# First 16 scores of each token found in the score stage, and 54 instead of 60 expert blocks ahead

## The chip, the cores and the metric

One core of one Trainium2 chip runs the whole program in one launch. The metric is device time in microseconds (us): 3645.66 us is the median of three runs before the change (3639.0 to 3648.67).

The engines are PE (TensorE matmul; PEld its weight loads), DVE (VectorE), ACT (ScalarE), POOL (GpSimd) and SP (SyncE, which only issues DMAs here). Each has its own instruction stream, runs it in order, and waits on semaphores for the others.

## The reference, cut to what matters

Two transformer blocks on 512 tokens of width 1024. All of the change lies in the last part, the PEER layer (a product-key mixture of 16384 experts):

```
def one(xb):                                   # 128 tokens
    q = (xb @ w_pq).reshape(128, 8, 2, 128)
    s = einsum('thpd,hpkd->thpk', q, sub_keys)             # 16 score rows of 128 keys per token
    sv, si = top_k(s, 16)                                  # "the first 16 scores"
    cand = sv[:, :, 0, :, None] + sv[:, :, 1, None, :]
    cidx = si[:, :, 0, :, None] * 128 + si[:, :, 1, None, :]
    best, pos = top_k(cand, 16)
    eidx = take_along_axis(cidx, pos);  g = softmax(best)
    act = gelu(einsum('thkd,td->thk', expert_u[eidx], xb))
    return einsum('thk,thkd->td', g * act, expert_v[eidx])
```

Here t is the token, h one of 8 heads, p the half of the key, k the key.

## The kernel before, in words

Matmuls are made of three: an f32 operand is split into hi and lo parts, and hi*hi, lo*hi and hi*lo are added in PSUM (lines 124 to 126). A weight tile of 128x1024 (512 KB) comes from DRAM into a ring of six `raw` buffers (`wload`, line 114), ACT casts the hi part (`whi`, line 117), and DVE or POOL subtracts it for the lo part (`wlo`, line 118). `whi` and `wlo` have three buffers each.

PEER has three stages.

- **The score stage** (`scores`). 16 blocks of `w_pq` are projected (24 matmuls of 512 columns each). `keys(m, q)` multiplies each q with its 128 sub-keys (four matmuls, one for each tile of 128 tokens), ACT copies the scores from PSUM to `psc`, and they are written to DRAM (`scd`). From the fifth block on, the residual is transposed and stored beside it.
- **The route stage** (`route`, with `up` beside it). For each of the four token tiles the 2048 scores of a token are read back (`sc`), and `top16` finds the first 16 of each of the 16 rows: MAX8, FIND_INDEX8, MATCH_REPLACE8, MAX8, FIND_INDEX8, all on DVE. Then come 50 candidate sums per head, their 16 best (`v3`), and `pick`, which turns positions into expert numbers (fi, fj) and gates. For tile 0 the expert rows themselves are gathered later. For tiles 1 to 3 the gates become dense: 32 groups a tile, each of four tokens, in which DVE writes one-hots `oj` and `oi` (for one group in four ACT scales `oi`) and PE multiplies them; ACT copies the result to `stage`. The generator yields at places where `peer` then writes an expert block ahead (`up`): projection of tiles 1 to 3 with `uT[i]` (24 matmuls of 384 columns), Gelu on ACT, result to DRAM (`actd`). NPRE = 60 blocks are done so. The 20 blocks that belong to top16's yields have their `wlo` subtraction on POOL, the other 40 on DVE.
- **The main loop**, 128 iterations. Iteration i multiplies the gated activations of block i with `v[i]` (`down`, 18 matmuls of 512 columns). An activation is either read back (`mixed`, i < NPRE; called a plain iteration below) or computed then with `up` two iterations ahead (called a mixed iteration: 42 matmuls). Beside it the 256 gathered rows of tile 0 (128 of u, 128 of v, 512 KB each for 128 tokens, in the same `raw` ring) are fetched by POOL's indirect DMAs and reduced on DVE: one an iteration up to NPRE, and the rest spread evenly over what is left (`want`).

The order of instructions on each engine is made by the framework's scheduler when the program is built; the source gives what depends on what, and the buffers. Memory pools matter too: `pe` (which holds `act` and `stage`) is opened after `pq`, the score stage's pool, is closed, and takes its place in SBUF.

Of the kernel before, what the change touches and what calls it, by code (L numbers as in the profile page):

```python
# [7 lines left out]
F32 = mybir.dt.float32  # L8
F32R = mybir.dt.float32r
I32 = mybir.dt.int32  # L10
U32 = mybir.dt.uint32
# [4 lines left out]
P = 128  # L16
# [11 lines left out]
class Kern:  # L28
# [1536 lines left out]
    def peer(self, h, first, residual, done):  # L1565

        nc, a = self.nc, self.a
        mod = self.mod2
        hhi, hlo = h
        with ExitStack() as c:  # L1570
            p0 = self.pool(c, "pe0")
            h0 = self.h0 = self.t(p0, [P, D], "h0")
            with ExitStack() as c1:
                qp = self.pool(c1, "pq")
                self.sk = self.t(qp, [P, 16, P], "sk")
                nc.sync.dma_start(self.sk, a["sk"])
                self.scores(qp, hhi, hlo, first, residual)
                done()
            pp = self.pool(c, "pe")
            self.stage = self.t(pp, [P, 2, P, 64], "stage")  # L1580
            with ExitStack() as c2:
                rp = self.pool(c2, "pr")
                self.iota16 = self.t(rp, [P, 16], "iota")
                nc.sync.dma_start(self.iota16, a["iota16"])
                self.iota = self.t(rp, [P, P], "iota128")
                nc.sync.dma_start(self.iota, a["iota128"])
                self.row0 = self.t(rp, [P, 16], "row0")
                nc.sync.dma_start(self.row0, a["row0"])
                jobs = self.route(rp, pp)
                pre = 0  # L1590
                for n, eng in jobs:
                    for _ in range(n):
                        if pre < self.NPRE:
                            self.up(pp, pre, hhi, hlo, eng)
                            pre += 1
# [27 lines left out]
            for t in range(4):  # L1623
                for i in range(2):
                    s = slice(512 * i, 512 * i + 512)
# [3 lines left out]
                    else:  # L1629
                        z = self.raw()[:, :512]  # L1630
# [3 lines left out]

    NPRE = 60
    PROD = 5
# [9 lines left out]
    def scores(self, p, hhi, hlo, first, residual):  # L1646

        nc, a = self.nc, self.a

        def keys(m, q):  # L1650
            pk = self.mm_ps()
            for t in range(4):
                nc.tensor.matmul(pk[:, t * P : t * P + P], q[:, t * P : t * P + P], self.sk[:, m], start=True, stop=True)
            s = self.t(p, [P, 4, P], "psc", bufs=2)
            nc.scalar.copy(s, pk.rearrange("p (t k) -> p t k", t=4))
            nc.sync.dma_start(a["scd"].rearrange("t p m k -> p t m k")[:, :, m], s)

        h = list(zip(hhi, hlo))
        qs = [self.t(p, [P, S], "pq", bufs=3) for _ in first]
        self.halves(first, h, lambda n, ps, cs: nc.scalar.copy(qs[n][:, cs], ps[:, cs]), lambda i: None)  # L1660
        last = list(enumerate(qs))
        norm = self.last_hi, self.last_split
        for m in range(len(first), 16):
            with self.after(*norm):
                w = self.cut(*self.wload(a["w_pq"][m]))
            ps = self.mm_ps()
            self.proj_feat(w, h, ps)
            for z in last:
                keys(*z)
            q = self.t(p, [P, S], "pq", bufs=3)  # L1670
            nc.scalar.copy(q, ps)
            last = [(m, q)]
            if 4 <= m < 12:
                with self.after(*norm):
                    residual(m - 4)
        keys(*last[0])
# [10 lines left out]
    def route(self, p, pp):  # L1687

        nc, a = self.nc, self.a
        dve, pool = nc.vector, nc.gpsimd  # L1690
        for t in range(4):
            sc = self.t(p, [P, 16, P], "sc", bufs=1)
            nc.sync.dma_start(sc, a["scd"][t])
            sv = self.t(p, [P, 16, 16], "sv", bufs=1)
            si = self.t(p, [P, 16, 16], "si", U32, bufs=1)
            for m in range(16):
                self.top16(p, sc[:, m], P, sv[:, m], si[:, m], "v2")
                if m % 4 == 3:
                    yield 1 + (t == 0), pool
            sf = self.t(p, [P, 16, 16], "sf", bufs=1)  # L1700
# [14 lines left out]
            for h in range(8):  # L1715
                self.top16(p, cand[:, h], 50, best[:, h], pos[:, h], "v3")
            yield 2, dve
            pf = self.t(p, [P, 8, 16], "pf", bufs=1)
# [19 lines left out]
            self.pick(p, pf, self.iota16, f4[:, :, 1], fj, ALU.is_equal)  # L1738
            yield 2, dve
            g = self.t(pp, [P, 8, 16], "gate0") if t == 0 else self.t(p, [P, 8, 16], "gate", bufs=1)  # L1740
            nc.vector.tensor_sub(g, best, best[:, :, 0:1].to_broadcast([P, 8, 16]))
            nc.scalar.activation(g, g, AF.Exp)
            s = self.t(p, [P, 8], "gs", bufs=1)
# [11 lines left out]
            tp = self.sc_ps()  # L1755
# [3 lines left out]
            for b in range(32):  # L1759
# [18 lines left out]
                if b % 4 == 3:  # L1778
                    yield 1, dve
                if t < 3 and b % 16 == 15:  # L1780
# [100 lines left out]
    def scratch(self):  # L1881
# [3 lines left out]
        self.a["growd"] = dp.tile([1, D], F32, tag="growd", name="growd")  # L1885
        self.a["scd"] = dp.tile([4, P, 16, P], F32, tag="scd", name="scd")
        self.a["gd"] = dp.tile([4, P, P, 64], F32, tag="gd", name="gd")
# [152 lines left out]
```

## Time and profile before

| | |
|---|---|
| median of the runs | 3645.66 us |
| profiled execution, its own time | 3644.18 us |
| its span (first to last instruction) | 3642.1 us |
| busy share of the span: PE, PEld, DVE, ACT, POOL | 96%, 83%, 72%, 44%, 21% |
| moved from and to HBM | 566.66 MB read, 41.18 MB written |

The profiled execution lies 1.5 us under the median. PE is busy nearly all the time, but a busy PE is not PE at its peak: matmuls are pipelined, so what counts is how many of them a stretch holds. The stages of PEER by the trace: the score stage ends at 2371 us, the route stage at 2759 us, the main loop at about 3634 us.

### The profile page before, as it was taken

What the parts mean: (1) busy time and instruction counts of PE and PEld (TensorE: products, weight loads), DVE (VectorE), ACT (ScalarE), POOL (GpSimd) and SP (SyncE); (2) the same over time, 40 slices, a digit from 0 to 9 for tenths busy, and PEclk for the clock granted to TensorE, in tenths of its full rate; (3) what the DMA queues carried; (4) which work ended last, traced back from release to release, by engine and by line L of the source; (5) the groups of instructions that cost most, each with busy time, mean ns of one, the idle gap of its engine ahead of it and who ended that gap; (6) DMA issues with size and microseconds to landing.
All of it is one profiled execution on the core that took longest, in us unless ns stands there. A gap on an engine that the chain in (4) does not pass through costs nothing.

```text
span 3642.1 us, 53180 instructions
## 1 busy us (share of the span) xinstructions
PE 3505.6 (96%) x19035; PEld 3036.0 (83%) x19035; DVE 2624.4 (72%) x6192; ACT 1590.9 (44%) x3137; POOL 774.2 (21%) x890
## 2 busy tenths in 40 slices
PE   6999999999999999999999999999988999999998
PEld 5899888888888987888888768889987888788787
DVE  6788677874478864488736675189998887777777
ACT  4676533413367754342334554334554333333332
POOL 4223101000232320010012212021101223333232
PEclk9999999999999999999999999999999999999999
DMA  5211266673321122446632112455556998888887
GB/s 197 70 37 56 77 202 203 219 237 103 107 70 60 53 70 70 143 147 219 204 122 65 56 39 102 140 175 165 200 180 219 336 329 290 294 308 301 294 290 267
DMA packets 228821, 611.33 MB, mean 168 GB/s; under 512 B 24070, under 2 KB 89638, under 8 KB 225868
## 3 DMA queue, kind: packets, MB, share of 16 engines
q1 hardware_dynamic: 191692, 473.69, 39.1%
q0 software_dynamic: 36864, 134.23, 11.1%
q8 instruction: 150, 2.46, 0.3%
q14 instruction: 115, 0.94, 0.1%
HBM read 566.66 MB, written 41.18 MB: 167 GB/s over the span
## 4 chain that ended last, share of the span: by engine, by line
PE 67%; DVE 13%; DMA 12%; ACT 4%; issue 3%; POOL 0%; SPq 0%; DVEq 0%; ACTq 0%; POOLq 0%
PE mm L124 16%; PE mm L125 16%; PE mm L126 16%; DMA raw<-uT 8%; DVE wlo L118 4%; DMA raw<-v 3%; ACT whi L117 3%; PE pv L552 1%; DVE oi L1773 1%; PE tr L126 1%; PE tr L124 1%; PE tr L125 1%; PE sc L496 1%; PE mm L1775 1%; DVE oj L1765 1%
## 5 line engine op out<-in xcount | busy, mean ns | idle before, releaser
L117 ACT CAST whi<-raw 128x1024 fp32r<-128x1024 f32 (+2 forms) x603 | 610.2, 1015 | 1153.5 <-PE mm L125 411.5
L118 DVE TENSOR_TENSOR wlo<-raw,whi 128x1024 fp32r<-128x1024 f32 (+2 forms) x583 | 686.8, 1180 | 445.6 <-ACT whi L117 383.6
L126 PE MATMUL tr<-hhi,wlo 128*128 128x384 f32 x1024 | 356.4, 348 | 24.1 <-DVE wlo L118 23.7
L124 PE MATMUL tr<-hhi,whi 128*128 128x384 f32 x1024 | 353.0, 345 | 18.0 <-ACT whi L117 13.6
L124 PE MATMUL mm<-hhi,whi 128*128 128x512 f32 (+1 forms) x976 | 366.6, 376 | 0.2 <-ACT mr L746 0.2
L125 PE MATMUL mm<-hlo,whi 128*128 128x512 f32 (+1 forms) x976 | 363.6, 373 | 1.8 <-DVE hlo L153 1.2
L126 PE MATMUL mm<-hhi,wlo 128*128 128x512 f32 (+1 forms) x976 | 363.2, 372 | 0.0
L125 PE MATMUL tr<-hlo,whi 128*128 128x384 f32 x1024 | 349.4, 341 | 0.0
L124 PE MATMUL mm<-whi,hhi 128*128 128x384 f32 (+2 forms) x896 | 308.6, 345 | 21.1 <-ACT hhi L152 13.7
L229 DVE CUSTOM_DVE_ANT_0 adaj<-adaw,cr 128x256 f32<-128x256 f32 x620 | 271.5, 438 | 57.4 <-DMA adaw<-ada_w 43.8
L125 PE MATMUL mm<-wlo,hhi 128*128 128x384 f32 (+2 forms) x896 | 308.4, 344 | 2.8 <-DVE wlo L118 2.8
L126 PE MATMUL mm<-whi,hlo 128*128 128x384 f32 (+2 forms) x896 | 305.9, 342 | 0.0
L282 POOL TENSOR_TENSOR nsum<-nsum,nsq 128x256 f32<-128x256 f32 x78 | 68.9, 887 | 1099.7 <-ACT nsq L280 1098.1
L1848 POOL DMA_INDIRECT raw<-u,idx x128 | 144.9, 1132 | 460.1 <-DVE act L1856 320.3
L126 PEld LDWEIGHTS tr<-hhi,wlo 128*128 128x128 f32 x1024 | 196.0, 191 | 40.9 <-DVE wlo L118 39.7
L124 PEld LDWEIGHTS tr<-hhi,whi 128*128 128x128 f32 x1024 | 196.4, 192 | 31.1 <-ACT whi L117 23.4
L125 PEld LDWEIGHTS mm<-hlo,whi 128*128 128x128 f32 x976 | 183.8, 188 | 34.0 <-DVE hlo L153 1.7
L124 PEld LDWEIGHTS mm<-hhi,whi 128*128 128x128 f32 x976 | 183.6, 188 | 33.5 <-issue 0.7
L126 PEld LDWEIGHTS mm<-hhi,wlo 128*128 128x128 f32 x976 | 183.7, 188 | 32.5 <-issue 0.3
L124 PEld LDWEIGHTS mm<-whi,hhi 128*128 128x128 f32 x896 | 171.6, 191 | 37.2 <-ACT hhi L152 13.8
L125 PE MATMUL mm<-wlo,ewh 128*128 128x512 f32 x512 | 201.4, 393 | 0.0
L126 PE MATMUL mm<-whi,ewl 128*128 128x512 f32 x512 | 199.6, 392 | 0.0
(602 smaller groups left out, 8390.1 us busy)
## 6 DMA issues: line engine op xcount, KB each, us to landing
adaw<-ada_w SPq DMA_DIRECT2D x139, 512.0 KB
raw<-uT SPq DMA_DIRECT2D x128, 512.0 KB
raw<-v SPq DMA_DIRECT2D x128, 512.0 KB
raw<-w_up SPq DMA_DIRECT2D x64, 512.0 KB
raw<-w_dn SPq DMA_DIRECT2D x64, 512.0 KB
raw<-w_b SPq DMA_DIRECT2D x48, 384.0 KB
raw<-w_aqk SPq DMA_DIRECT2D x32, 512.0 KB
raw<-w_g SPq DMA_DIRECT2D x32, 512.0 KB
```

The source lines that it names most:

```text
L117: nc.scalar.copy(hi[:, :n], raw[:, :n])
L118: self.last_lo = (eng or nc.vector).tensor_sub(lo[:, :n], raw[:, :n], hi[:, :n])
L124: mm(ps, ah, bh, start=start, stop=False)
L125: mm(ps, ah, bl, start=False, stop=False)
L126: mm(ps, al, bh, start=False, stop=stop)
L229: nc.vector.tensor_tensor_reduce(junk, wt[:, q * 256 : q * 256 + 256], cond[:, q * 256 : q * 256 + 256], op0=ALU.mult, op1=ALU.add, scale= ...
L282: add_ins = (nc.vector if k == 7 else nc.gpsimd).tensor_add(tot, tot, sq)
L496: self.nc.tensor.matmul(ps, q, hi, start=True, stop=False)
L552: nc.tensor.matmul(po[:, cols], wT[:, kt], v[:, kt, hl * P : hl * P + P], start=(kt == 0), stop=(kt == 3))
L1765: nc.vector.tensor_tensor(oj, io, cb(1), ALU.is_equal)
L1773: nc.vector.tensor_scalar(oi[:, n], self.iota, one(0), one(2), ALU.is_equal, ALU.mult)
L1848: nc.gpsimd.indirect_dma_start(z, None, src, bass.IndirectOffsetOnAxis(ap=idx[:, k % P : k % P + 1], axis=0))
```

## The change

`psc` is no longer written to DRAM and read back. `keys` calls `top16` on the four tiles of `psc` as soon as they are in SBUF, and the results of all four tiles are kept in `tops`. The sub-keys come in 16 loads of 64 KB (three buffers) in place of one of 1 MB. The `wlo` subtractions of `w_pq` (14 of the 16 blocks) go from DVE to POOL, those of all `up` blocks to DVE. NPRE is 54, the yields hand out 6, 14, 14 and 20 blocks to the four tiles, and the pool `pe` lies on the other side of SBUF.

```diff
--- before.py
+++ after.py
@@ -1570,15 +1570,16 @@
         with ExitStack() as c:
             p0 = self.pool(c, "pe0")
             h0 = self.h0 = self.t(p0, [P, D], "h0")
+            c2 = ExitStack()
+            tp = self.pool(c2, "pt")
+            self.tops = [(self.t(tp, [P, 16, 16], "sv", bufs=4), self.t(tp, [P, 16, 16], "si", U32, bufs=4)) for _ in range(4)]
             with ExitStack() as c1:
                 qp = self.pool(c1, "pq")
-                self.sk = self.t(qp, [P, 16, P], "sk")
-                nc.sync.dma_start(self.sk, a["sk"])
                 self.scores(qp, hhi, hlo, first, residual)
                 done()
-            pp = self.pool(c, "pe")
+            pp = self.pool(c, "pe", side="right")
             self.stage = self.t(pp, [P, 2, P, 64], "stage")
-            with ExitStack() as c2:
+            with c2:
                 rp = self.pool(c2, "pr")
                 self.iota16 = self.t(rp, [P, 16], "iota")
                 nc.sync.dma_start(self.iota16, a["iota16"])
@@ -1588,10 +1589,10 @@
                 nc.sync.dma_start(self.row0, a["row0"])
                 jobs = self.route(rp, pp)
                 pre = 0
-                for n, eng in jobs:
+                for n in jobs:
                     for _ in range(n):
                         if pre < self.NPRE:
-                            self.up(pp, pre, hhi, hlo, eng)
+                            self.up(pp, pre, hhi, hlo)
                             pre += 1
             while pre < self.NPRE:
                 self.up(pp, pre, hhi, hlo)
@@ -1632,7 +1633,7 @@
                         (nc.vector if 2 * t + i > 4 else nc.gpsimd).tensor_add(xt[t][:, s], xt[t][:, s], z)
                     nc.sync.dma_start(a["out"][t * P : t * P + P, s], xt[t][:, s])
 
-    NPRE = 60
+    NPRE = 54
     PROD = 5
     BOUND = (6, 14), (3, 8)
     BOUND2 = (6, 14), (8, 17)
@@ -1649,11 +1650,14 @@
 
         def keys(m, q):
             pk = self.mm_ps()
+            sk = self.t(p, [P, P], "sk", bufs=3)
+            nc.sync.dma_start(sk, a["sk"][:, m])
             for t in range(4):
-                nc.tensor.matmul(pk[:, t * P : t * P + P], q[:, t * P : t * P + P], self.sk[:, m], start=True, stop=True)
+                nc.tensor.matmul(pk[:, t * P : t * P + P], q[:, t * P : t * P + P], sk, start=True, stop=True)
             s = self.t(p, [P, 4, P], "psc", bufs=2)
             nc.scalar.copy(s, pk.rearrange("p (t k) -> p t k", t=4))
-            nc.sync.dma_start(a["scd"].rearrange("t p m k -> p t m k")[:, :, m], s)
+            for t in range(4):
+                self.top16(p, s[:, t], P, *(z[:, m] for z in self.tops[t]), "v2")
 
         h = list(zip(hhi, hlo))
         qs = [self.t(p, [P, S], "pq", bufs=3) for _ in first]
@@ -1662,7 +1666,7 @@
         norm = self.last_hi, self.last_split
         for m in range(len(first), 16):
             with self.after(*norm):
-                w = self.cut(*self.wload(a["w_pq"][m]))
+                w = self.cut(*self.wload(a["w_pq"][m], eng=nc.gpsimd))
             ps = self.mm_ps()
             self.proj_feat(w, h, ps)
             for z in last:
@@ -1687,16 +1691,8 @@
     def route(self, p, pp):
 
         nc, a = self.nc, self.a
-        dve, pool = nc.vector, nc.gpsimd
         for t in range(4):
-            sc = self.t(p, [P, 16, P], "sc", bufs=1)
-            nc.sync.dma_start(sc, a["scd"][t])
-            sv = self.t(p, [P, 16, 16], "sv", bufs=1)
-            si = self.t(p, [P, 16, 16], "si", U32, bufs=1)
-            for m in range(16):
-                self.top16(p, sc[:, m], P, sv[:, m], si[:, m], "v2")
-                if m % 4 == 3:
-                    yield 1 + (t == 0), pool
+            sv, si = self.tops[t]
             sf = self.t(p, [P, 16, 16], "sf", bufs=1)
             nc.vector.tensor_copy(sf, si)
 
@@ -1714,7 +1710,7 @@
             pos = self.t(p, [P, 8, 16], "pos", U32, bufs=1)
             for h in range(8):
                 self.top16(p, cand[:, h], 50, best[:, h], pos[:, h], "v3")
-            yield 2, dve
+            yield 2 + (t == 0)
             pf = self.t(p, [P, 8, 16], "pf", bufs=1)
             nc.vector.tensor_copy(pf, pos)
 
@@ -1736,7 +1732,7 @@
             nc.vector.tensor_sub(pf, pf, df)
             fj = self.t(p, [P, 8, 16], "fj", bufs=1)
             self.pick(p, pf, self.iota16, f4[:, :, 1], fj, ALU.is_equal)
-            yield 2, dve
+            yield 4 - (t == 0)
             g = self.t(pp, [P, 8, 16], "gate0") if t == 0 else self.t(p, [P, 8, 16], "gate", bufs=1)
             nc.vector.tensor_sub(g, best, best[:, :, 0:1].to_broadcast([P, 8, 16]))
             nc.scalar.activation(g, g, AF.Exp)
@@ -1776,7 +1772,7 @@
                 st = self.stage[:, b // 16]
                 nc.scalar.copy(st[:, :, 4 * (b % 16) : 4 * (b % 16) + 4], ps.rearrange("p (t i) -> p i t", t=4))
                 if b % 4 == 3:
-                    yield 1, dve
+                    yield 1 + (t == 3 and b > 8)
                 if t < 3 and b % 16 == 15:
                     for q in range(4):
                         nc.sync.dma_start(a["gd"][2 * (t - 1) + b // 16, :, 32 * q : 32 * q + 32], st[:, 32 * q : 32 * q + 32, :])
@@ -1883,7 +1879,6 @@
         self.a["xs"] = dp.tile([8, P, S], F32, tag="xs", name="xs")
         self.a["x2"] = dp.tile([4, P, D], F32, tag="x2", name="x2")
         self.a["growd"] = dp.tile([1, D], F32, tag="growd", name="growd")
-        self.a["scd"] = dp.tile([4, P, 16, P], F32, tag="scd", name="scd")
         self.a["gd"] = dp.tile([4, P, P, 64], F32, tag="gd", name="gd")
         self.a["actd"] = dp.tile([self.NPRE, P, 384], F32, tag="actd", name="actd")
         self.a["rows"] = dp.tile([4, 8, P], F32, tag="rows", name="rows")
```

The scheduler makes these orders of it. DVE, at the end of the norm (`hlo`) that comes ahead of the score stage's first keys. Before, the subtractions of `w_pq` follow:

```order
L153 TENSOR_TENSOR hlo_22608<-nh_22357,hhi_22600 128x256
L118 TENSOR_TENSOR wlo_22785<-raw_22782,whi_22784 128x1024
L118 TENSOR_TENSOR wlo_22834<-raw_22831,whi_22833 128x1024
L118 TENSOR_TENSOR wlo_22875<-raw_22872,whi_22874 128x1024
L118 TENSOR_TENSOR wlo_22927<-raw_22924,whi_22926 128x1024
```

Of the change, the first scores' top16 (`psc_22828` and `psc_22861` are the scores of keys 0 and 1, `sv` and `si` the values and indices of the four tiles):

```order
L153 TENSOR_TENSOR hlo_22607<-nh_22356,hhi_22599 128x256
L1685 MAX sv_22632<-psc_22828 128x8
L1685 MAX sv_22634<-psc_22828 128x8
L1685 MAX sv_22636<-psc_22828 128x8
L1685 MAX sv_22638<-psc_22828 128x8
L1686 MAX_INDEX si_22633<-sv_22632,psc_22828 128x8
L1687 MATCH_REPLACE v_4697_22830<-sv_22632,psc_22828 128x128
L1685 MAX sv_22632<-psc_22861 128x8
```

All 320 top16 instructions of the 64 rows stand in DVE's stream from here on; 240 of them come ahead of the first `wlo` of a block ahead.

POOL, at the same place in the program. Before, the 20 subtractions of blocks ahead begin here (`raw_23522` holds the first `uT`):

```order
L153 TENSOR_TENSOR hlo_22609<-nh_22358,hhi_22601 128x256
L118 TENSOR_TENSOR wlo_23525<-raw_23522,whi_23524 128x1024
L118 TENSOR_TENSOR wlo_23559<-raw_23556,whi_23558 128x1024
L118 TENSOR_TENSOR wlo_23617<-raw_23614,whi_23616 128x1024
L118 TENSOR_TENSOR wlo_23651<-raw_23648,whi_23650 128x1024
```

Of the change, the 14 of `w_pq` (`raw_22790` holds `w_pq[2]`), and nothing of the blocks ahead:

```order
L153 TENSOR_TENSOR hlo_22608<-nh_22357,hhi_22600 128x256
L118 TENSOR_TENSOR wlo_22793<-raw_22790,whi_22792 128x1024
L118 TENSOR_TENSOR wlo_22892<-raw_22889,whi_22891 128x1024
L118 TENSOR_TENSOR wlo_22958<-raw_22955,whi_22957 128x1024
L118 TENSOR_TENSOR wlo_23035<-raw_23032,whi_23034 128x1024
```

So each subtraction has changed its engine with one of the other kind.

PE, at the end of the route stage: the last matmuls of the last block ahead (`tr`) and the one-hot groups (`mm<-oi,oj`) behind them. Before:

```order
L1775 MATMUL mm_26218<-oi_26220,oj_26219 128x128 x4
L126 MATMUL tr_27615<-hhi_22600,wlo_27612 128x384
L124 MATMUL tr_27615<-hhi_22601,whi_27611 128x384
L125 MATMUL tr_27615<-hlo_22609,whi_27611 128x384
L126 MATMUL tr_27615<-hhi_22601,wlo_27612 128x384
L1775 MATMUL mm_26231<-oi_26233,oj_26232 128x128 x4
L1775 MATMUL mm_26244<-oi_26246,oj_26245 128x128 x4
L1775 MATMUL mm_26291<-oi_26293,oj_26292 128x128 x4
```

Of the change:

```order
L124 MATMUL tr_27419<-hhi_22600,whi_27415 128x384
L125 MATMUL tr_27419<-hlo_22608,whi_27415 128x384
L126 MATMUL tr_27419<-hhi_22600,wlo_27416 128x384
L1771 MATMUL mm_26963<-oi_26965,oj_26964 128x128 x2
L1771 MATMUL mm_26977<-oi_26979,oj_26978 128x128
L1771 MATMUL mm_26963<-oi_26965,oj_26964 128x128
```

Before, 42 groups (ten of tile 2 and all 32 of tile 3) come behind the last block ahead; of the change, 16 groups of tile 3 do.

## Rows read from the trace of the kernel before

**Rows 1.** Stretches: window, length, busy us (instructions) by engine, clock, DMA, GB/s.

```profile
2280.00:2371.00 91.00, 91.00 (x481) 78.31 (x479) 12.25 (x10) 32.26 (x55) 7.20 (x3) 1.00 0.50 146
2371.00:2378.00 7.00, 5.39 (x28) 4.54 (x26) 0.69 (x1) 3.19 (x5) 4.11 (x2) 1.00 0.60 205
2378.00:2529.00 151.00, 140.61 (x771) 137.76 (x772) 150.70 (x709) 53.03 (x76) 33.81 (x12) 0.97 0.53 171
2529.00:2690.00 161.00, 157.89 (x1048) 157.29 (x1047) 160.65 (x466) 85.42 (x161) 14.72 (x8) 0.99 0.54 194
2690.00:2759.00 69.00, 53.08 (x354) 49.00 (x352) 67.60 (x183) 38.31 (x86) 0.00 (x0) 0.90 0.26 90
2759.00:3010.00 251.00, 246.30 (x1078) 202.84 (x1079) 208.02 (x360) 95.53 (x123) 62.00 (x59) 0.99 0.95 326
3010.00:3624.00 614.00, 579.92 (x2817) 508.14 (x2816) 464.06 (x602) 190.27 (x269) 204.42 (x195) 0.99 0.86 296
```

**Rows 2.** Waits in 2690 to 2760: engine line waited for, us, times, longest.

```profile
PE mm L1775 <- ACT oi L1771: 12.2, 10, 2.0
PE mm L1775 <- DVE oi L1773: 3.3, 8, 0.5
```

**Rows 3.** DVE in order of time, 2378 to 2405: start, us, what, count, [idle before].

```profile
2378.30 1.26 DVE L1681 MAX8 sv<-sc 128x8 f32<-128x128 f32 x6 [6.37 <-DMA sc<-scd]
...
2387.01 1.76 DVE L1708 TENSOR_TENSOR cand<-sv 128x64 f32<-128x64 f32 x5
2388.69 0.08 DVE L1683 MATCH_VALUE_LOAD v<-sv,sc 128x8 f32 x1
...
2398.46 0.20 DVE L1708 TENSOR_TENSOR cand<-sv 128x64 f32<-128x64 f32 x1
...
2403.34 1.22 DVE L118 TENSOR_TENSOR wlo<-raw,whi 128x1024 fp32r<-128x1024 f32 x1
2404.48 0.21 DVE L1684 MAX8 best<-v 128x8 f32<-128x50 f32 x1
```

**Rows 4.** Instructions of some tiles: count, ns min/median/max, first and last start.

```profile
L1681 DVE MAX8 sv<-sc x64: 270/277/296, 2378.3 to 2519.2; 128x8 f32<-128x128 f32 x64
L1685 DVE FIND_INDEX8 si<-sv,v x64: 274/281/305, 2385.8 to 2613.4; 128x8 uint32<-128x128 f32 x64
L1792 DVE TENSOR_TENSOR eq<-eq,d x8: 1211/1230/2926, 2425.6 to 2663.5; 128x1024 f32<-128x1024 f32 x8
L118 POOL TENSOR_TENSOR wlo<-raw,whi x20: 2339/2415/4484, 2352.8 to 2602.8; 128x1024 fp32r<-128x1024 f32 x20
```

**Rows 5.** Chain that ended last, 2330 to 2560: start, us, what.

```profile
2338.59 0.89 PE mm L1653 x8
2345.50 0.89 PE mm L1653 x8
2351.85 0.89 PE mm L1653 x8
...
2529.31 2.68 PE mm L1775 x24
```

**Rows 6.** Short stretches: route stage, plain iterations, mixed iterations (columns as in Rows 1).

```profile
2384.00:2399.00 15.00, 15.00 (x88) 15.00 (x87) 15.00 (x101) 5.75 (x8) 7.20 (x3) 1.00 0.34 103
2850.00:2900.00 50.00, 50.00 (x222) 41.41 (x221) 42.33 (x75) 19.11 (x25) 13.00 (x13) 1.00 0.98 342
3400.00:3500.00 100.00, 92.95 (x443) 81.76 (x443) 75.58 (x86) 29.39 (x42) 30.60 (x32) 0.97 0.84 286
```

**Rows 7.** One-hot matmuls alone (line 1775): length, PE busy (count), PEld busy (count).

```profile
2529.00:2690.00 161.00, 56.96 (x424) 55.61 (x424) 0.99 0.54 194
2690.00:2759.00 69.00, 51.91 (x345) 47.98 (x344) 0.90 0.26 90
```

**Rows 8.** Start of the score stage in order of time: POOL, ACT.

```profile
2266.76 2.37 POOL L153 TENSOR_TENSOR hlo<-nh,hhi 128x256 fp32r<-128x256 f32 x3
2267.94 2.95 ACT L117 CAST whi<-raw 128x1024 fp32r<-128x1024 f32 x3
```

**Rows 9.** Mixed iterations, 3010 to 3642: longest wait; then the chain's shares, 3010 to 3624.

```profile
ACT whi L117 <- DMA raw<-uT: 402.3, 66, 7.9
...
by line: DMA raw<-uT 48.9%; DVE wlo L118 16.4%; ACT whi L117 11.4%; issue 8.1%; DMA raw<-v 6.8%; DVE ewl L153 3.6%; DVE h L1869 1.2%; PE tr L126 0.9%; PE tr L125 0.7%; PE tr L124 0.7%; PE mm L124 0.4%; PE mm L125 0.4%; PE mm L126 0.4%; DVE 
```

## The prediction

> **What bounds the kernel now.** First the slices of the page: nothing before 2260 us is touched, since only PEER's code changes, so I read PEER by stretches [rows 1]. The score stage (to 2371) is PE's: 91.00 busy of 91 us, DVE 12.25. The route stage (2371 to 2759) is DVE's: 150.70 of 151, 160.65 of 161 and 67.60 of 69 us. PE's busy figure hides how far it is from its peak, so I count matmuls. A matmul of a block ahead costs 15.00/87 = 0.172 us when nothing holds PE up [rows 6], a one-hot matmul 2.68/24 = 0.112 us [rows 5]. In 2378 to 2529 PE's 771 matmuls need 133 of 151 us (88%); in 2529 to 2690, 424 one-hots [rows 7] and 624 others need 155 of 161 us (96%); in 2690 to 2759, 344 one-hots need 38.5 of 69 us (56%). That last stretch is the tail in which no block ahead is left and PE waits for one-hots, which DVE writes and ACT scales [rows 2].
>
> The main loop has two paces. A plain iteration takes 18 x 50/222 = 4.05 us with PE full [rows 6]; a mixed one 42 x 614/2817 = 9.15 us [rows 1], where PE alone would need 18 x 0.225 + 24 x 0.172 = 8.2. There ACT waits 402.3 us for `uT` to land, and the chain has 48.9% of 614 us in that transfer [rows 9].
>
> **The change part by part**
>
> *The sets leave the route.* From 2378.30 to 2398.46 DVE does the 16 first top16 sets and 1.68 us of `cand` (2387.01 to 2388.69) [rows 3]: (20.16 - 1.68)/16 = 1.155 us a set, 64 sets are 73.9 us. (Adding the instructions' durations would count more: they overlap.) Back come 14 more subtractions on DVE (54 now, 40 before), at 2404.48 - 2403.34 = 1.14 us [rows 3], 16.0 us. DVE's route: 378.95 - 73.9 + 16.0 = 321 us. Two-input operations that ran into POOL's subtractions were longer (2926 against 1230 ns [rows 4]); with 16 subtractions in that stage and at most 1.7 us each, 0 to 27 us of the 321 may go as well. I take 0, because PE decides below.
>
> *The sets in the score stage.* A block there takes PE 6.35 to 6.91 us [rows 5]; its four sets take DVE 4.62 us. Added waits: ACT's copy into `psc` waits for the sets two blocks back, and behind it on ACT stands the next `whi` cast, for which PE waits. With 4.62 under 6.35 it doesn't bite. The last keys' sets end some 5 us after PE, at 2376; before, DVE began at 2378.30, after the scores had gone through DRAM. Cost 0; from below -2, from above the rival on the sets.
>
> *`w_pq` on POOL.* 2.4 us in place of 1.14 [rows 4] against a block of 6.35 us, three buffers deep: hidden. The first subtraction can start when POOL's `hlo` ends at 2269.13 and the cast at 2268.9 [rows 8], so is 1.3 us later than DVE's; PE reads the lo part last of the three. Cost 0 to 1.3, I take 0. *Sub-keys in 16 loads*: each waits on SP for the keys three blocks back; queued behind it are loads of `w_pq` and `uT` and the residual's stores. The `scd` writes stood in the same places and waited for a later event (the copy of the newest scores), so SP gets no slower. Cover if not: the `raw` ring of six, some 40 us of blocks. The 8.4 MB of `scd` traffic that go lie in stretches with DMA at 0.50 to 0.54 [rows 1]: nothing.
>
> *The route's new length.* In both orders the first block ahead stands beside the last keys, before 2371. Then 53 blocks of 24 matmuls, 53 x 24 x 0.172 = 218.8 us, and the 80 groups that stand before the last block's end, 80 x 8 x 0.112 = 71.7 us: 290.5 us at PE's peak. DVE has 321 less the tail's share in the same time, so the two are nearly equal, as in 2529 to 2690. I take that stretch's 96%: 302 us. Ends: 290 (100%) and 331 (88%, the first stretch). Then the tail of 16 groups at 69/43 = 1.6 us [rows 7], set by DVE: 25.7 us. The route ends at 2371 + 302 + 26 = 2699 in place of 2759: **-60 us** (-72 to -31). DVE's own sum, 2376 + 321 = 2697, says the same.
>
> *Six blocks move into the loop.* Six iterations turn from plain into mixed. Upper end: each costs the mean difference, 6 x (9.15 - 4.05) = 31 us. Lower end by the ring: gathered rows per mixed iteration fall from 196/66 = 2.97 to 202/72 = 2.81, raw tiles from 4.97 to 4.81; were the pace per tile, an iteration would take 8.86 us, and 73 x 8.86 - 67 x 9.15 - 6 x 4.05 = +9 us. By bytes alone (0.524 MB of `uT` for 0.197 of `actd`, 2 MB at 296 GB/s) +7. Since half the chain is the landing of `uT`, which fewer rows shorten only in part, I take the middle: **+20 us**.
>
> Sum against the profiled execution's 3644.2 us: 3644.2 - 60 + 20 = 3604; the median lies 1.5 us higher, so **3606 us**.
>
> **A rule on POOL beside DVE.** The rows: 16 subtractions of POOL ran in the same stretches as the sets, and no MAX8 or FIND_INDEX8 took over 305 ns against medians near 280, while `eq`, with two inputs, went to 2926 [rows 4]. The Trainium skill, "SBUF — State Buffer", section "Who interferes with whom", says that a DVE instruction with one SBUF input outside the two-port modes does not meet POOL, and one with two does, the later of the two blocked altogether. By it the sets lose nothing beside the 14 subtractions, and the sum stays 3606; if they were blocked as `eq` was, it would be the rival on the sets, 3620. The trace agrees with it so far, and that rival's chance is halved by it.
>
> **The rivals**
>
> *PE starves in the route* (chance 0.18). PE and DVE with nearly the same work wait for each other at every chore of 10 us that DVE puts between two subtractions; PE then keeps the first stretch's 88% to the end. For it: that stretch, whose DVE stream looks the same as what is left of it. Against: there DVE had 20% more to do than PE. Route -31, loop +20: 3634.
>
> *The loop takes the six blocks cheaply* (0.12). Early mixed iterations run near PE's 8.2 us and the thinner gathering lets the ring run ahead. Route -60, loop +7: 3592. Against: the waits for `uT` in nearly every mixed iteration [rows 9].
>
> *The sets pace the score stage* (0.05): the work moves but doesn't vanish. If POOL's 2.40 us block the sets once a block, DVE needs 4.62 + 2.40 = 7.02 us a block against 6.35 to 6.91; 16 blocks end at some 2385, and 14 us of sets stay in the route: 3620.
>
> *Slower: the loop's mixed pace gives way* (0.06). Place: the `raw` ring and the transfers behind it. The route's 60 us are lost when 73 mixed iterations take over (613 + 24 + 60)/73 = 9.55 us on average. For it: the slowest window runs at 42 x 100/443 = 9.48 [rows 6], and the six new ones add `uT` loads to a DMA share of 0.86. Against: fewer gathered rows in each. At 9.8 us the loop gains 78 us: 3664.
>
> **How the numbers follow.** The forecast has 0.59, its own range 3593 to 3621 (loop +9 to +31, route -62 to -56). What a measurement of this kernel can tell from no change is about 0.3%, 11 us. Faster: the forecast, the cheap loop, the sets and half of the starved PE, 0.59 + 0.12 + 0.05 + 0.09 = 0.85. The other half of the starved PE is within: 0.09. Slower 0.06. The range from 3580 (the route's best end, -72, with a cheap loop) to 3636 (the starved PE) leaves out some 0.15.
>
> **What would show it.** Right: a score stage still at 91 us with DVE some 70% busy; no idle DVE behind it; the tail without `tr` at some 26 us; the loop beginning some 60 us earlier; plain iterations at 4.05 us, six fewer, and mixed ones at 8.9 to 9.1. Wrong: blocks of over 7 us in the score stage (the sets), a count of matmuls in the route that needs under 90% of its time (starved PE), or a mixed mean above 9.5 us.

## The result and the profile after

The changed kernel takes 3599.2 us (median of 4 runs, 3591.2 to 3604.0) against 3643.4 us (4 runs): ratio 0.987, 95% interval 0.985 to 0.989. 3606 us were predicted, with a range of 3580 to 3636. The profiled execution, the fastest of the four, took 3591.2 us (span 3589.4).

Below, "before" is the kernel before and "after" the changed one. The stretches of after, in the columns of [rows 1] (length, busy us and instructions of PE, PEld, DVE, ACT, POOL, then clock, DMA share, GB/s); the line of 321 us is the whole route stage, and the last a stretch of plain iterations alone:

```profile
2280.00:2371.00 91.00, 91.00 (x478) 78.23 (x477) 74.31 (x483) 32.07 (x56) 25.09 (x11) 1.00 0.34 108
2371.00:2379.00 8.00, 5.52 (x30) 4.69 (x29) 8.00 (x39) 4.25 (x6) 0.00 (x0) 1.00 0.18 66
2379.00:2464.00 85.00, 85.00 (x484) 84.93 (x483) 84.62 (x317) 38.07 (x53) 0.00 (x0) 0.98 0.52 168
2464.00:2650.00 186.00, 186.00 (x1275) 185.90 (x1274) 174.12 (x430) 105.10 (x204) 3.80 (x4) 1.00 0.57 203
2650.00:2667.00 17.00, 17.00 (x122) 17.00 (x121) 14.24 (x40) 8.72 (x19) 0.61 (x1) 1.00 0.51 169
2667.00:2692.00 25.00, 19.69 (x149) 18.18 (x147) 23.99 (x69) 14.63 (x34) 0.00 (x0) 1.00 0.08 25
2692.00:2920.00 228.00, 223.88 (x979) 184.86 (x980) 188.45 (x326) 87.97 (x113) 57.93 (x54) 0.99 0.95 325
2920.00:3575.00 655.00, 627.75 (x3079) 554.72 (x3078) 495.99 (x647) 209.02 (x293) 224.37 (x200) 0.99 0.86 293
...
2371.00:2692.00 321.00, 313.21 (x2052) 310.70 (x2050) 304.97 (x889) 170.76 (x314) 4.40 (x4) 0.99 0.50 174
...
2850.00:2900.00 50.00, 50.00 (x222) 41.44 (x221) 42.86 (x74) 19.46 (x26) 12.09 (x12) 1.00 0.96 326
```

The first line is the score stage: its length and PE's 91.00 us are what they were, while DVE went from 12.25 to 74.31 us. The next four are the route up to its last block ahead: 296 us from 2371 to 2667, with PE busy in nearly all of it and DVE below full from 2464 on (174.12 of 186 us). The line of 25 us is the tail. Over the whole route DVE is busy for 304.97 of 321 us. Of the one-hot matmuls alone (line 1771 now; the two columns are PE and PEld):

```profile
2464.00:2667.00 203.00, 83.47 (x632) 82.02 (x632) 1.00 0.56 200
2667.00:2692.00 25.00, 17.87 (x136) 16.52 (x136) 1.00 0.08 25
```

By the count of [rows 6] and [rows 5], 632 of the 1397 matmuls (1275 + 122) in 2464 to 2667 are one-hots: 632 x 0.112 + 765 x 0.172 = 202 of 203 us. In 2379 to 2464, 484 x 0.172 = 83 of 85 us. So PE is fed to 98% or more, where the kernel before had 88% and 96%.

The sets in their new place, DVE in order of time (start, us, what, [idle before]):

```profile
2340.15 0.87 DVE L1685 MAX8 sv<-psc 128x8 f32<-128x128 f32 x4 [2.15 <-ACT psc L1658]
...
2344.65 0.28 DVE L1689 FIND_INDEX8 si<-sv,v 128x8 uint32<-128x128 f32 x1
...
2347.07 0.87 DVE L1685 MAX8 sv<-psc 128x8 f32<-128x128 f32 x4 [2.14 <-ACT psc L1658]
```

A block takes 2347.07 - 2340.15 = 6.92 us, its four sets 2344.93 - 2340.15 = 4.78, and then DVE waits 2.1 us for the next scores. PE's chain does not know of them:

```profile
2303.67 0.89 PE mm L1656 x8
2310.58 0.89 PE mm L1656 x8
```

6.91 us apart, as the longer step in [rows 5]. Durations of single instructions, to hold against [rows 4]:

```profile
L1685 DVE MAX8 sv<-psc x64: 273/276/296, 2279.6 to 2371.5; 128x8 f32<-128x128 f32 x64
L1687 DVE MATCH_REPLACE8 v<-sv,psc x64: 272/276/283, 2280.7 to 2376.2; 128x128 f32<-128x128 f32 x64
L1689 DVE FIND_INDEX8 si<-sv,v x64: 282/285/297, 2284.2 to 2378.3; 128x8 uint32<-128x128 f32 x64
...
L1788 DVE TENSOR_TENSOR eq<-eq,d x8: 1209/1218/1225, 2394.2 to 2550.0; 128x1024 f32<-128x1024 f32 x8
...
L124 PE MATMUL sc<-whi,ewh x256: 387/389/628, 2698.5 to 3577.7; 128*128 128x512 f32 x128
```

The longest `eq` took 2926 ns before and takes 1225 ns now: no POOL subtraction is left beside it. The last row gives the main loop, two such matmuls an iteration, first start to last: 879.2 us. In before the same row is

```profile
L124 PE MATMUL sc<-whi,ewh x256: 387/389/527, 2765.0 to 3630.9; 128*128 128x512 f32 x128
```

865.9 us. So the loop begins 66.5 us earlier and lasts 13.3 us longer: -53.2, which is the difference of the two profiled executions (3591.2 - 3644.2 = -53.0). Waits of after, in the stretches 2379 to 2667, 2667 to 2692 and 2920 to 3575 (us, times, longest):

```profile
DVE oj L1761 <- PE mm L1771: 8.1, 11, 1.5
...
PE mm L1771 <- ACT oi L1767: 3.9, 3, 1.5
PE mm L1771 <- DVE oi L1769: 1.3, 3, 0.5
...
ACT whi L117 <- DMA raw<-uT: 391.5, 70, 8.5
```

The first shows which engine is ahead: DVE now waits for PE, so from 2464 on PE is the bound of the route. In the tail PE still waits for one-hots, less than in [rows 2]. The last is the loop's wait of [rows 9], nearly as long as it was. The chain by engine says the same of the whole span (PE had 67% and DVE 13% before):

```profile
PE 75%; DMA 11%; DVE 7%; ACT 4%; issue 2%; POOL 1%; DVEq 0%; SPq 0%; ACTq 0%; POOLq 0%
```

### The profile page after: what moved, and what is told of

Its sections match the earlier page's. It is cut to its first block, busy times and chain, and to the rows that moved or that the text cites. A ratio compares the mean times of both kernels' runs of the same rounds, so it can differ in the third digit from the quotient of the medians.

```text
span 3589.4 us, 53133 instructions
## 1 busy us (share of the span) xinstructions
PE 3483.3 (97%) x19035; PEld 3023.3 (84%) x19035; DVE 2619.7 (73%) x6198; ACT 1592.9 (44%) x3137; POOL 766.1 (21%) x884
## 4 chain that ended last, share of the span: by engine, by line
PE 75%; DMA 11%; DVE 7%; ACT 4%; issue 2%; POOL 1%; DVEq 0%; SPq 0%; ACTq 0%; POOLq 0%
PE mm L124 17%; PE mm L125 16%; PE mm L126 16%; DMA raw<-uT 8%; DVE wlo L118 3%; ACT whi L117 3%; PE tr L126 2%; PE tr L124 2%; PE tr L125 2%; DMA raw<-v 2%; PE mm L1771 2%; PE pv L552 1%; PE sc L496 1%; PE sc L497 1%; PE sc L124 1%
## 5 line engine op out<-in xcount | busy, mean ns | idle before, releaser
L118 DVE TENSOR_TENSOR wlo<-raw,whi 128x1024 fp32r<-128x1024 f32 (+2 forms) x589 | 694.6, 1181 | 387.6 <-ACT whi L117 375.4
```

The source lines that it names most:

```text
L118: self.last_lo = (eng or nc.vector).tensor_sub(lo[:, :n], raw[:, :n], hi[:, :n])
```

## The experiments

Each run has a median of its own and a ratio to the kernel before on the same chip, with its 95% interval. For the steps I compare profiled executions by the row of `sc` shown above: its first start is the loop's start, and last less first the loop's length. One profiled execution can lie up to 14 us off the median of its run, so totals are compared by medians.

| profiled execution | loop starts | last `sc` | length | mixed iterations |
|---|---|---|---|---|
| before | 2765.0 | 3630.9 | 865.9 | 68 |
| before, `wlo` all on DVE | 2767.8 | 3633.8 | 866.0 | 68 |
| before, 54 ahead | 2759.3 | 3647.3 | 888.0 | 74 |
| after, 60 ahead | 2721.5 | 3578.0 | 856.5 | 68 |
| after | 2698.5 | 3577.7 | 879.2 | 74 |
| after, 48 ahead | 2686.7 | 3595.7 | 909.0 | 80 |
| after, sets twice | 2742.8 | 3634.6 | 891.8 | 74 |
| after, `w_pq` on DVE | 2698.0 | 3579.3 | 881.3 | 74 |
| after, `up` partly on POOL | 2708.5 | 3588.7 | 880.2 | 74 |
| after, ACT every second | 2693.9 | 3584.7 | 890.8 | 74 |
| after, rows spread | 2697.8 | 3589.4 | 891.6 | 74 |
| after, ring of seven | 2707.4 | 3580.1 | 872.7 | 74 |
| after, own `v` buffers | 2705.0 | 3570.9 | 865.9 | 74 |
| both last gains | 2690.8 | 3548.3 | 857.5 | 74 |

### The sets without the shift: 60 blocks ahead in the changed kernel

```diff
-    NPRE = 54
+    NPRE = 60
-                    yield 1 + (t == 3 and b > 8)
+                    yield 1 + (t == 2 and b > 8) + (t == 3 and b > 8)
```

> The change with 60 blocks ahead again (the sets stay in the score stage; the last two tiles hand out six more blocks, and no one-hot group is left behind the last block). Theory A (with the sets gone PE sets the route, and the loop pays 13 us for six blocks, as the two traces show): route 59 x 4.13 + 96 x 0.89 = 329 us of matmuls at 98% = 336, ends at 2707 in place of 2692, +15; loop -13: about 3601, no change, so that the shift of six blocks is worth nothing by itself. Rival B (the shift of blocks made the gain): back to the old number of blocks gives back over half of it, 3620 or more. Rival C (DVE still sets the route): 6 x 1.14 = +7 there, -13 in the loop, 3593.

Measured: 3599.1 us, ratio 0.988 (0.986 to 0.990), the time of the changed kernel. The gain doesn't need the six blocks; it comes from the rest of the change, which is the sets with their other edits. The two halves of the shift show in the table: the route 23.0 us longer (2721.5 - 2698.5), the loop 22.7 shorter. Both were expected smaller (+15 and -13), and the sum was met because the two errors cancel. The end of the route in that kernel:

```profile
2464.00:2667.00 203.00, 203.00 (x1396) 202.97 (x1395) 190.22 (x470) 115.91 (x226) 0.00 (x0) 1.00 0.56 201
2667.00:2692.00 25.00, 25.00 (x179) 25.00 (x179) 22.41 (x55) 15.03 (x31) 3.44 (x3) 1.00 0.34 113
```

PE goes on full where the changed kernel has its tail; six blocks of 24 matmuls at 0.172 us are 24.8 us of PE, and PE pays them in the route as it would in the loop.

### The shift without the sets: 54 blocks ahead in the kernel before

```diff
-    NPRE = 60
+    NPRE = 54
```

> The kernel before with 54 blocks ahead, nothing else (sets in the route stage, POOL's subtractions there). Theory A: DVE is the route's bound, and six blocks fewer take only 6 x 1.14 = 7 us off it; 56 one-hot groups stand behind the last block. Loop +13: 3649, not faster. Rival B (fewer blocks ahead make the gain): PE's 6 x 4.13 = 25 us come off the route, less 13 in the loop: 3631.

Measured: 3664.5 us, ratio 1.006 (1.004 to 1.007), slower by 21 us, and 15 us above the 3649 that theory A gave. The route gets only 5.7 us shorter, the loop 22.1 longer, where +13 was expected. The route there is DVE's, and a block ahead costs DVE only its subtraction. The six blocks dropped are the last six, and all of theirs are DVE's (POOL has its 20 as before): 6 x 1.14 = 6.8 us. The shift is a loss where DVE is the bound and neutral where PE is.

### Six blocks more into the loop: 48 ahead

```diff
-    NPRE = 54
+    NPRE = 48
-                    yield 1 + (t == 3 and b > 8)
+                    yield 1
```

> The change with 48 blocks ahead (the last tile hands out 8 in place of 14). Theory A: 34 groups are left behind the last block, at 1.6 us by DVE 54 us; ahead of it 47 x 4.13 + 62 x 0.89 = 249 us at 98%, route ends at 2371 + 254 + 54 = 2679, -13; loop +13: 3599, no change. Rival B (each six blocks shifted are worth what the PE time in the route says): -25 + 13, 3587. Rival D (the loop takes further blocks at the full difference of plain and mixed, 6 x 5.1 = 31): 3617.

Measured: 3608.6 us, ratio 0.991 (0.989 to 0.993): 9 us above the changed kernel, where no change was expected. Route -11.8, about as expected, but loop +29.8, near rival D's 31 and not the 13 of theory A. The route has come back to DVE at its end:

```profile
2464.00:2655.00 191.00, 184.29 (x1264) 182.66 (x1264) 179.76 (x459) 105.80 (x211) 5.65 (x4) 0.99 0.54 193
2655.00:2680.00 25.00, 19.14 (x135) 17.57 (x134) 24.94 (x71) 14.08 (x32) 0.00 (x0) 0.93 0.00 1
```

PE lost 6.7 of 191 us where it had lost none. Six blocks are 24.8 us of PE, of which the route keeps 11.8. Between 54 and 60 the balance is flat; at 48 it is worse.

### The sets twice

```diff
             for t in range(4):
                 self.top16(p, s[:, t], P, *(z[:, m] for z in self.tops[t]), "v2")
+                self.top16(p, s[:, t], P, *(z[:, m] for z in self.tops[t]), "v2")
```

> The change with each first top16 set in the score stage done twice (same inputs, same outputs). Theory A (the sets are hidden there because DVE needs 4.6 us a block and PE 6.35 to 6.9; beyond that they set the pace): 9.2 us a block, 16 blocks take some 148 us from 2280, the score stage ends near 2410 to 2428 in place of 2371, 40 to 55 us later: 3640 to 3655. Rival (DVE's idle time in the score stage, 27 us, and in the route, 16 us, takes most of the second sets): 74 - 43 = 31 us, 3630.

Measured: 3645.8 us, ratio 1.000 (0.999 to 1.001), 46 us above the changed kernel.

```profile
2280.00:2371.00 91.00, 87.96 (x443) 74.18 (x442) 91.00 (x612) 27.58 (x46) 24.98 (x11) 0.98 0.31 96
2371.00:2430.00 59.00, 44.90 (x224) 40.55 (x223) 59.00 (x346) 18.33 (x26) 0.00 (x0) 0.83 0.31 101
```

DVE is full through both stretches and PE, starved, is busy for 44.90 of 59 us in the second. The granted clock of that row is 0.83. The second copy's 64 x 1.195 = 76 us find 17 us of room in the score stage (91.00 - 74.31) and 16 us in the route (321 - 304.97); the 43 to 44 us left come out on the path, and the loop starts 44.3 us later. This bears out that the first copy is free because it fits into DVE's idle time in the score stage.

### `w_pq` on DVE

```diff
-                w = self.cut(*self.wload(a["w_pq"][m], eng=nc.gpsimd))
+                w = self.cut(*self.wload(a["w_pq"][m]))
```

> The change with the subtractions of w_pq on DVE again, beside the sets, and POOL idle in the score stage. Theory A (DVE has room in the score stage): 4.62 + 1.14 = 5.76 us a block against 6.35, no change, 3599. Rival (the subtraction queues behind up to four sets on DVE, and PE waits for the lo part): 14 blocks at 1 to 2 us, 3613 to 3627.

Measured: 3594.7 us, ratio 0.987 (0.985 to 0.989): no difference.

```profile
2280.00:2371.00 91.00, 91.00 (x482) 78.62 (x481) 85.08 (x488) 32.25 (x56) 0.00 (x0) 1.00 0.37 111
```

DVE has 85.08 of 91 us to do and PE is still full. The move to POOL was neither needed nor harmful, as far as these runs can tell.

### A third of the `up` subtractions on POOL

```diff
-                            self.up(pp, pre, hhi, hlo)
+                            self.up(pp, pre, hhi, hlo, nc.gpsimd if pre % 3 == 2 else None)
```

> The change with every third subtraction of a block ahead on POOL (18 of 54), as the kernel before had 20 of 60. Theory A (PE sets the route now and is fed at 98%): DVE loses 20 us of work that nobody waited for, and the two-input operations run into POOL's subtractions again: 3599 to 3607. Rival C (DVE is still half the bound): up to 16 us less, 3585.

Measured: 3609.6 us, ratio 0.991 (0.989 to 0.992): 10 us above the changed kernel.

```profile
2379.00:2464.00 85.00, 81.06 (x448) 79.99 (x449) 84.58 (x307) 35.64 (x50) 17.30 (x6) 0.96 0.49 151
...
2371.00:2703.00 332.00, 317.60 (x2053) 311.54 (x2051) 320.48 (x878) 170.63 (x317) 58.95 (x23) 0.99 0.49 169
...
L1788 DVE TENSOR_TENSOR eq<-eq,d x8: 1197/1208/3179, 2393.0 to 2545.7; 128x1024 f32<-128x1024 f32 x8
```

In the same 85 us PE gets 448 matmuls in place of 484; DVE is as full as in after, with fewer instructions (307 for 317). Taking subtractions off DVE does not feed PE better; the loop starts 10.0 us later. Over the whole route (second line) DVE is even busy for longer, 320.48 us for the 304.97 of after, though 18 subtractions have left it: beside POOL's subtractions the longest `eq` takes 3179 ns again, for 1225. So with the sets gone, keeping these subtractions on DVE is worth some 10 of the 44 us.

### The kernel before with all subtractions on DVE

```diff
-                            self.up(pp, pre, hhi, hlo, eng)
+                            self.up(pp, pre, hhi, hlo)
```

> The kernel before with all 60 subtractions of blocks ahead on DVE and none on POOL in the route. Theory A (DVE's sum sets that route): 16 x 1.14 = 18 us more on DVE, less some 13 us by which its two-input operations ran into POOL's: +5, 3648. Rival E (what starved PE in the route before were POOL's slow subtractions, not DVE's sets): the route gains the 12% that PE missed in its first stretch, 18 us: 3626.

Measured: 3647.5 us, ratio 1.001 (1.000 to 1.002), some 5 us slower, as theory A has it: that part of the change brings nothing without the move of the sets.

```profile
2378.00:2529.00 151.00, 146.88 (x825) 145.88 (x825) 148.69 (x684) 55.05 (x76) 0.00 (x0) 0.98 0.57 183
```

PE gets 825 matmuls here against 771 in [rows 1], but DVE has the same list plus the subtractions that were POOL's, and the loop starts 2.8 us later.

### Rows spread over more of the loop

```diff
-    EARLY = 2
+    EARLY = 6
```

> The change with the gathered rows spread over 68 mixed iterations in place of 72 (2.97 a mixed iteration, the rate of the kernel before), and none left for the last six. Theory ring (a mixed iteration is paced by the number of raw tiles it takes): 68 at 9.15 and 6 at 8.3 us in place of 74 at 8.95, +10: 3609. Theory landing (the transfer of uT sets the pace whatever is gathered): no change, 3599.

Measured: 3599.6 us, ratio 0.987 (0.986 to 0.989): no change. The loop's wait stays:

```profile
ACT whi L117 <- DMA raw<-uT: 412.6, 70, 7.6
```

The theory of the ring would have cost 10 us, which the medians don't show, so the lower end that I had for the loop (8.86 us by tiles of the ring) had no ground. A smaller effect isn't excluded: this execution's loop, 891.6 us, is at the upper end of what the same loop takes elsewhere.

### A ring of seven

```diff
-    RING = 6
+    RING = 7
-            s = self.t(p, [P, 4, P], "psc", bufs=2)
+            s = self.t(p, [P, 4, P], "psc", bufs=1)
-        qs = [self.t(p, [P, S], "pq", bufs=3) for _ in first]
+        qs = [self.t(p, [P, S], "pq", bufs=2) for _ in first]
-            q = self.t(p, [P, S], "pq", bufs=3)
+            q = self.t(p, [P, S], "pq", bufs=2)
```

> The change with a raw ring of seven buffers in place of six, in the SBUF that the 1 MB of sub-keys no longer takes (psc has one buffer and pq two to make room). Theory landing (a mixed iteration waits for uT because its load can only be issued when a raw buffer comes free): the load goes out one buffer earlier, some 1.8 us, and the 48 us that 74 mixed iterations lose against 8.3 us shrink by half or more: 3570 to 3580. Rival bandwidth (the DMA engines at 0.86 are the limit): no change, 3599; or slower by the score stage, if one psc buffer is too few.

Measured: 3593.0 us (3576.9 to 3597.0), ratio 0.984 (0.982 to 0.987). The wait for `uT`, 391.5 us in after, goes down:

```profile
ACT whi L117 <- DMA raw<-uT: 307.8, 71, 7.3
```

The loop is 6.5 us shorter than that of after (872.7). The gain in the median is as small, and the intervals overlap. That is less than the 3570 to 3580 of the theory of landing, though a fifth of the wait is gone: the length of this wait is not what it costs.

### Two raw buffers of its own for `v`

```diff
-        raw = self.raw()
+        raw = self.raw() if src is not self.vsrc else self.t(self.vp, [P, 1024], "vraw", bufs=2)
-        w = self.t(self.vp, [P, 3, P], "ew", bufs=2)
+        w = self.t(self.vp, [P, 3, P], "ew", bufs=1)
-        vh, vl = self.wload(a["v"][i], pool=self.vp, bufs=2)
+        self.vsrc = a["v"][i]
+        vh, vl = self.wload(self.vsrc, pool=self.vp, bufs=2)
```

> The change with two raw buffers of its own for v in the main loop (ew has one buffer to make room), so that the ring of six serves uT and the gathered rows alone. Nothing ahead of the loop is touched. Theory landing: v and uT no longer wait for each other's buffers, uT is issued earlier, and of the some 50 us that the mixed iterations lose against 8.3 us half or more go: 3565 to 3575. Rival bandwidth (DMA share 0.86 is the limit whenever the loads are issued): no change, 3599.

Measured: 3571.9 us (3560.9 to 3585.6), ratio 0.980 (0.978 to 0.982): 27 us faster than the changed kernel.

```profile
2920.00:3300.00 380.00, 377.41 (x1891) 342.92 (x1890) 297.21 (x423) 127.75 (x178) 162.42 (x123) 0.99 0.88 308
3300.00:3540.00 240.00, 227.05 (x1110) 200.46 (x1109) 179.35 (x206) 76.26 (x106) 100.02 (x75) 0.99 0.83 291
```

The same two stretches of after:

```profile
2920.00:3300.00 380.00, 365.17 (x1800) 323.11 (x1799) 283.46 (x404) 120.78 (x169) 136.82 (x118) 1.00 0.86 294
3300.00:3540.00 240.00, 228.14 (x1113) 201.51 (x1112) 183.75 (x209) 76.37 (x107) 77.28 (x74) 0.99 0.86 292
```

Over the first 380 us PE is busy in all but 2.6, and a mixed iteration takes 42 x 380/1891 = 8.44 us, near the 8.2 that PE alone needs, against 42 x 380/1800 = 8.87 in after. Behind 3300 nothing is gained (1110 matmuls for 1113), and why is open. The wait for `uT` is 307.1 us here, as with the ring of seven. DMA moves 308 GB/s in the first stretch where it moved 294, so the memory was not at its limit in after. That `uT` was late there because the shared ring held back its issue is the likely reason, but these views don't show it by themselves.

The traces hold only part of the 27 us. The loop is 13.3 us shorter than in after, or 19 against the average of the five executions named below. This profiled execution is the slowest of its five (3585.6 us): it is 9 us behind after when the score stage begins (first `psc` at 2287.7 us for 2279.0), ahead of which the edit touches nothing.

### ACT scales every second group

```diff
-                if b % 4 == 0:
+                if b % 2 == 0:
-                    if b % 4 == 0:
+                    if b % 2 == 0:
```

> The change with every second one-hot group's oi scaled by ACT in place of every fourth. Theory A (the tail behind the last block ahead is DVE's): a group costs DVE 1.42 us on average in place of 1.63, the tail of 25 us shrinks by some 3 to 10 us (the scheduler leaves 7 groups behind the last block in place of 16), but with 54 blocks PE's sum bounds it: 3590 to 3596. Rival (PE's sum is all that counts from 2371 to the loop): 3599.

Measured: 3591.8 us, ratio 0.985 (0.984 to 0.987); the interval overlaps that of the changed kernel, and the loop of this execution (890.8 us) hides the gain in its total. The row of the one-hots (first and last start) shows the step by itself, here and below it in after:

```profile
L1771 PE MATMUL mm<-oi,oj x768: 270/275/377, 2465.1 to 2686.8; 128*128 128x128 f32 x192
L1771 PE MATMUL mm<-oi,oj x768: 270/275/377, 2464.8 to 2691.7; 128*128 128x128 f32 x192
```

From first to last it is 221.7 us for 226.9: the end of the route comes 5 us earlier.

### Both together

> The changed kernel with both edits that gained alone: two raw buffers of its own for v in the main loop (alone 3571.9 us), and ACT scaling the one-hots of every second group in place of every fourth (alone 3591.8 us against 3599.2 to 3599.6). Theory A, the two gains lie in different stages, the route (DVE's tail and chores) and the loop (the wait for uT to land), and add up: 3571.9 - 7 = about 3565 us, 3560 to 3570. Theory B, ACT is what the loop's first iterations wait for once the v loads are out of the way, or the earlier end of the route only moves the loop against its transfers, which set its pace: the 7 us are lost, 3572 us.

Measured: 3563.0 us (3558.9 to 3574.9, 5 runs), ratio 0.978 (0.976 to 0.981), the lowest median of all: 81 us under the kernel before. 9 us lie between it and the one without ACT's part, where 7 were expected from adding up. Steps of that size are within what the runs scatter, and the two intervals overlap, so the times alone don't show that the gains add up. But the row of the one-hots shortens by 5.2 us in both pairs of traces (here 2464.3 to 2686.0, without ACT's part 2473.5 to 2700.4).

```profile
2905.00:3250.00 345.00, 344.15 (x1735) 312.08 (x1734) 273.17 (x398) 118.61 (x165) 154.35 (x113) 1.00 0.88 312
```

42 x 345/1735 = 8.35 us a mixed iteration: this part of the loop is PE's.

## Why the prediction was right

*The sets leave the route.* Right: -60 us predicted, -66.5 in the traces. The term is a little mis-sized, and its own range (-62 to -56) misses it: I took for PE the 96% from 2529 to 2690 of the kernel before, a stretch in which DVE was full, and it was 98%, 290.5/296. (The row behind the 0.172 has 88 matmuls and not 87, which makes it 0.170 and takes some 2 us off the 290.) The tail's 25.7 us were 25. I had PE and DVE nearly equal and no idle DVE behind the score stage. That holds for the first 85 us alone; from 2464 on DVE waits for PE, and DVE's route, for which I had 321 us, is at most 304.97. The likely reason is the term of 0 to 27 us that I put at 0: two-input operations beside POOL's subtractions. The kernel before with all subtractions on DVE points the same way: the loop starts only 2.8 us later with some 18 us of subtractions more.

*The sets cost nothing in the score stage.* Shown from both sides: the stage's length is the same, with DVE at 82% and with `w_pq` added at 93%; with the sets twice the excess comes out on the path. My "some 70%" was too low: the scores of the first two keys come together, so nearly all 64 sets fall into the 91 us, at 1.195 us each. The room was 17 us, less than I had thought.

*`w_pq` on POOL, sub-keys in 16 loads.* 0 and 0. The first is shown by its own run. The loads were not tried alone; PE's 91.00 us of the score stage leave them no cost there.

*Six blocks into the loop.* +20 predicted. The pair of traces gives +13.3, but five executions with the same loop (after, sets twice, `w_pq` on DVE, `up` partly on POOL, ACT every second) have 879.2 to 891.8 us, 884.7 on average, +19 against before. The mixed iteration's 8.93 us lies in the 8.9 to 9.1 that I gave. What I did not see is that the shift is not needed: of the route's 66.5 us, 23 are the six blocks' own work, which the loop pays back. With them left ahead the route gains 43.5 and the loop 9.4, and the time is the same.

*The sum.* 3644.2 - 66.5 + 13.3 = 3591 in the profiled execution; with the loop's average, 3597, beside the median of 3599.2. The 7 us between 3606 and the median are for the most part the route's term.

*The rivals.* PE starving in the route (3634): refuted by 98%. The loop taking the blocks cheaply (+7, 3592): the pair of traces alone (+13.3) lies between it and the forecast, but the other four executions (+14.3 to +25.9) and the three shifts of six blocks (+22.7, +22.1, +29.8) speak against it. Sets pacing the score stage: refuted by 6.92 us a block, of which they fill 4.78. That a DVE instruction with one SBUF input, outside the two-port modes, does not meet POOL (the Trainium skill, "SBUF — State Buffer", section "Who interferes with whom") agrees with this trace: POOL is busy for 25.09 us in that stage, and the longest MAX8 took 296 ns. The mixed pace giving way: 8.93 us against the break-even of 9.55.

What stays open: why the same loop takes from 879 to 892 us in different executions; why with 60 blocks ahead it takes 9.4 us less than in before, with as many mixed iterations; and which part of the 27 us that the `v` buffers bring is the issue order and which the extra buffers. Only the ring of seven, smaller in its effect, stands beside it. The loads of sub-keys were not tried alone.

## What to carry to other kernels

Before pricing work that leaves a full engine, ask which engine is next and how much of its peak it already gets: here the route's gain ended where PE was fed, not at the 74 us taken off DVE. Work that moves from a stage where two engines are level into one that PE fills is only moved; price both ends, and try the move alone. A wait for a transfer with DMA at 0.86 need not be the memory's limit: look at which loads share a ring of buffers. Here two private buffers were worth more than half as much as the whole change by the medians, while one more shared buffer took as much off the wait and was worth 6 us.

## What the runs showed of the hardware

- MAX8, FIND_INDEX8 and MATCH_REPLACE8 of 128x128 overlap their neighbours: each takes 272 to 297 ns, four MAX8 in a row 0.87 us, and a set of five with their value loads 1.195 us in a row of four, where the five durations alone add up to 1.40.
- Taking a third of the `up` subtractions off DVE left PE with fewer matmuls (448 for 484 in 85 us) and DVE with more busy time (320.48 us of the route for 304.97). Two causes stand in the rows, and no run parts them: a subtraction takes 2.4 us on POOL for 1.14 on DVE [rows 4, 3], and beside it the longest `eq` takes 3179 ns for 1225.
- Two private buffers for `v` took 84 us off ACT's wait for `uT` (391.5 to 307.1) and 27 us off the median, with the DMA share near where it was (0.88 and 0.83 for 0.86). One more shared buffer took as much off the wait (307.8) and 6 us off the median.
